# The last LayerNorm of a decoder layer taken under the last two expert tiles, its shift written to the output early and its scaled rows added there by DMA

## The chip, the cores and the metric

One core of a Trainium2 chip runs the whole layer as one launch. The metric is the device time of that launch in microseconds (us), the median of several executions. One execution was taken with the hardware profiler; its span and its trace are what the rows below come from.

## The reference, cut to what matters

One decoder layer over 1024 tokens of 1024 float32 values. Two attention branches and an output projection come first, then a LayerNorm, then a mixture of 32 experts of which each token uses two (both in one group of eight), then the last LayerNorm:

```python
h = layer_norm(ALPHA * h + mix, ln1_g[l], ln1_b[l])
ffn = hierarchical_moe(h, moe_w_group[l], moe_b_group[l], moe_w_router[l], moe_b_router[l],
                       moe_w_gate[l], moe_w_up[l], moe_w_down[l])
h = layer_norm(ALPHA * h + ffn, ln2_g[l], ln2_b[l])
```

`layer_norm` takes mean and variance over the 1024 values of a row, scales by the gain `ln2_g` and adds the shift `ln2_b`. A row of the output can be normed only when both of its experts have been added to it.

## The kernel before, in words

The code does not issue instructions directly. Calls on `V` (VectorE), `S` (ScalarE), `G` (GpSimd), `PE` (TensorE) and `LD` (SyncE, which issues DMAs) are recorded as tasks, and a list scheduler, `Sched.flush`, puts them into one fixed order for each engine. Therefore nearly every row of a profile names line 312, and rows are told apart by the names of the tiles. On the chip an engine works through its order and waits wherever the next instruction must wait.

**The expert stage.** The rows after the first LayerNorm lie in DRAM twice: in `h1_d` (to be read) and in `y_d` (to be added to). Tile t takes one expert's tokens (up to 128). `gather_x` brings their rows in with an indirect DMA that GpSimd issues, `x_tr` transposes them, `gate_up`, `hidden`, `hid_tr` and `down` do the gated MLP, and `scatter` adds the result to `y_d` with an indirect DMA with `compute_op=add`, also issued by GpSimd. The four views of `y_d` let scatters of different expert groups go without waiting for one another; a tile of another kind uses `y_d` as a whole and waits for all earlier scatters to land. There are 33 tiles: 32 experts, and one overflow tile for tokens beyond the 128 of an expert. Its weights are fetched by indirect DMAs from GpSimd. Should more tiles overflow, a loop with a count read on the chip (`For_i`) runs after the stage; it runs zero times here.

The weights are float32. An expert has three chunks of 1 MB, loaded by SyncE into a ring of eight buffers `rw`. `w_split` makes a high and a low part of each half chunk: ScalarE copies (`whg`, `whd`), VectorE subtracts (`wlg`, `wld`). A chunk's buffer is free for the next load when that is done. In the loop over t the pass for t does `gate_up(t)`, `hid_tr` and `down` of tile p = t - 1, the splits of t + 1, and the scatter of tile p - 1.

**The last stage.** After tile 32, the overflow tile, has been scattered, eight tiles `z` of 128 rows are loaded from `y_d`. `z_in` takes mean and variance of each on VectorE or ScalarE, small operations on GpSimd, ScalarE and VectorE make the factor, `z_out` applies gain and shift in one of three ways, and SyncE stores the rows to the output. The gain and the shift (`lnr`, 2 times 512 KB as each partition gets its own copy) are loaded behind the last weights.

Of the kernel before, what the change touches and what calls it, by code (L numbers as in the profile page):

```python
# [12 lines left out]
F32 = mybir.dt.float32  # L13
# [419 lines left out]
def layer_kernel(ctx, tc, x, meta, cst, rope, lnrows, gcol, small, wr_in, w_in, w_uq, w_ukv, w_o, w_e, c_bd, c_key, c_mask, out):  # L433
# [21 lines left out]
    o_d = dram.tile([NB, 128, 2, 1024], F32, name="o_d")  # L455
    h1_d = dram.tile([NB * 128, D], F32, name="h1_d")
    y_d = dram.tile([NB * 128, D], F32, name="y_d")

    def st(shape, dt=F32, name="s", bufs=2):
        return sm.tile(shape, dt, name=name, tag=name, bufs=bufs)  # L460
# [855 lines left out]

    nload, nsplit = [0], [0]

    def expert(t):
        return t % 4 * 8 + t // 4  # L1320

    def load_chunk(e, c, after=None):
        i = nload[0]
        if RA + RX <= i < RA + RX + 4:
            RAW[e, c] = [pq4.tile([128, 1024], F32, name="w4", tag="w4", bufs=8) for _ in range(2)]
            parts = [(RAW[e, c][q], q * 1024, (q + 1) * 1024) for q in range(2)]
        else:
# [9 lines left out]
        if e < NE:  # L1337
# [306 lines left out]
    XS, YS, GU, HD, OV = ({} for _ in range(5))  # L1644

    def ix(t):
        e = expert(t) if t < NE else NE
        return slice(e, e + 1)

    def gather_x(t):  # L1650
# [43 lines left out]
    def down(t, q):  # L1694
        hh, hl = HD[t]
        y = ps.tile([128, 512], F32, name="y", tag="y", bufs=4)
        for f in range(2):
            hi, lo = WS[t, 4 + f]
            c = slice(q * 512, (q + 1) * 512)
            mm3(y, (hh[:, f, :], hl[:, f, :]), (hi[:, c], lo[:, c]), f == 0, f == 1)  # L1700
        if q == 0:
            YS[t] = pq4.tile([128, D], F32, name="w4", tag="w4", bufs=8)
        copy_s(YS[t][:, q * 512:(q + 1) * 512], y)

    def scatter(t):
        G.indirect_dma_start(out=View(y_d, t % 4, 4) if t < NE else y_d, out_offset=Offsets(idxX[:, ix(t)]), in_=YS.pop(t), in_offset=None,
                             bounds_check=NB * 128 - 1, oob_is_err=False, compute_op=OP.add)

    def overflow_table():
        f = pb.tile([128, 7, NE], F32, name="ovf", tag="ovf", bufs=1)  # L1710
# [42 lines left out]
        V.memset(prevk, -1.0)  # L1753

    NT = NE + 1
    for i in range(GB4):
        gather_x(i)
    for _ in range(RB):
# [7 lines left out]
    for t in range(NT + 1):  # L1766
        p = t - 1
        cur, nxt = t < NT, t + 1 < NT
        if cur:
            gate_up(t, 0)  # L1770
            if t:
                w_split(t, 5)
                load_more()
            gate_up(t, 1)
        if nxt and t:
# [21 lines left out]
            WS.pop((p, 4)), WS.pop((p, 5))  # L1797
        if t + LEAD < NT and t:
            gather_x(t + LEAD)
        if p >= 1:  # L1800
            scatter(p - 1)
        if nxt:
            w_split(t + 1, 3)
            load_more()
            w_split(t + 1, 4)
        if t == 12:
            overflow_list()
        if t == 16:
            overflow_table()
    Y = {NT - 1: YS[NT - 1].t}  # L1810
    scatter(NT - 1)
    XS[NT] = None
    lnr = rawp.tile([128, 2, D], F32, name="rw", tag="rw", bufs=RA)
    for q in range(2):
        LD.dma_start(lnr[:, q, :], bc_row(4 + q))
    sched.flush()
    sched.direct = True
    global NAMES
# [3 lines left out]
    with tc.For_i(0, n_more, 1):  # L1822
# [14 lines left out]
        down(t, 0)  # L1837
        down(t, 1)
        scatter(t)
    b1.close()  # L1840
    aw.close()
    sched.direct = False
    sched.clock = dict.fromkeys(sched.clock, max(t.end for t in Y[NT - 1].users) + 1.0)


    with ExitStack() as c1:
        pb = c1.enter_context(pool("f"))
        Z, CF = {}, {}
        for n in range(NB):
            Z[n] = pb.tile([128, D], F32, name="z", tag="z", bufs=8)  # L1850
            LD.dma_start(Z[n], y_d[n * 128:(n + 1) * 128, :])

        def small(name, *shape):
            return pb.tile([128] + list(shape), F32, name=name, tag=name, bufs=8)

        def z_in(n):
            z = Z[n]
            m, v, r, t, nm = (small(f"z{i}", 1) for i in range(5))
            if n in AS:
                acc = small("za", 2)  # L1860
                junk = pb.tile([128, D], F32, name="zj", tag="zj", bufs=2)
                S.activation(junk, z, AF.Copy, accum_out=acc[:, 0:1])
                G.tensor_scalar(m, acc[:, 0:1], -1.0 / D, None, op0=OP.mult)
                S.activation(junk, z, AF.Square, bias=m, accum_out=acc[:, 1:2])
                sched.late = -ZL
                G.tensor_scalar(v, acc[:, 1:2], 1.0 / D, LN_EPS / ALPHA ** 2, op0=OP.mult, op1=OP.add)
            else:
                s6 = small("zs", 2, 6)
                mv = small("zv", 2)
                for q in range(2):  # L1870
                    ln_stats(z, s6, q)
                V.bn_aggr(mv, flat(s6))
                sched.late = -ZL
                G.tensor_scalar(v, mv[:, 1:2], LN_EPS / ALPHA ** 2, None, op0=OP.add)
                G.tensor_scalar(m, mv[:, 0:1], -1.0, None, op0=OP.mult)
            S.activation(r, v, AF.Sqrt)
            V.reciprocal(r, r)
            G.tensor_scalar(t, r, r, v, op0=OP.mult, op1=OP.mult)
            G.tensor_scalar(t, t, -0.5, 1.5, op0=OP.mult, op1=OP.add)
            G.tensor_tensor(r, r, t, op=OP.mult)  # L1880
            if "A" in OUT[n][0][0] + OUT[n][1][0]:
                G.tensor_tensor(nm, m, r, op=OP.mult)
            sched.late = 0.0
            CF[n] = m, r, nm

        def z_out(n):
            z, (m, r, nm) = Z[n], CF[n]
            for q in range(2):
                c = slice(q * 512, (q + 1) * 512)
                way, e1, e2 = OUT[n][q]  # L1890
                g, b = lnr[:, 0, c], lnr[:, 1, c]
                if way == "A":
                    S.activation(z[:, c], z[:, c], AF.Identity, bias=nm, scale=r)
                    e1.tensor_tensor(z[:, c], z[:, c], g, op=OP.mult)
                    e2.tensor_tensor(z[:, c], z[:, c], b, op=OP.add)
                else:
                    V.scalar_tensor_tensor(z[:, c], z[:, c], m, g, op0=OP.add, op1=OP.mult)
                    if way == "B":
                        V.scalar_tensor_tensor(z[:, c], z[:, c], r, b, op0=OP.mult, op1=OP.add)
                    else:  # L1900
                        S.activation(z[:, c], z[:, c], AF.Copy, scale=r)
                        e2.tensor_tensor(z[:, c], z[:, c], b, op=OP.add)
                if n in HS:
                    LD.dma_start(out[n * 128:(n + 1) * 128, c], z[:, c])
            if n not in HS:
                LD.dma_start(out[n * 128:(n + 1) * 128, :], z)

        AS, HS, ZL, ZLAG = (2, 3, 5, 6, 7), (2, 3, 4, 5, 6, 7), 0.2, 3
        A, B, C = ("A", V, V), ("B", V, V), ("C", V, G)
        OUT = (C, B), (B, C), (B, C), (("A", G, G), B), (B, B), (B, B), (C, B), (B, A)  # L1910
        for i in range(NB + ZLAG):
            if i < NB:
                z_in(i)
            if i >= ZLAG:
                z_out(i - ZLAG)
    sched.flush()
    sched.direct = True


def _constants():  # L1920
# [79 lines left out]
```

## Time and profile before

| | |
|---|---|
| median of 3 runs | 915.42 us (915.32 to 917.07) |
| the profiled execution, its own time | 913.97 us |
| its span, first to last instruction | 912.2 us |
| TensorE busy | 802.9 us, 88% |
| VectorE busy | 671.9 us, 74% |
| ScalarE busy | 514.4 us, 56% |
| GpSimd busy | 339.6 us, 37% |

The profiled execution lies 1.45 us under the median, and its span is 1.77 us shorter than its own time. Busy shares are averages over stages that differ much: the experts take from about 505 us to 866 us of the span, the last stage the rest.

### The profile page before, as it was taken

The page shows a single profiled execution, that of the slowest core. Times are in us where ns is not written, and L with a number is a line of the kernel's source. Part 1 is how long each engine was busy: PE and PEld are TensorE (multiplying, and loading weights), DVE is VectorE, ACT ScalarE, POOL GpSimd, SP SyncE. Part 2 cuts the span into 40 slices and gives each one's busy share as a digit, 9 for nine tenths or more (in the row PEclk, how much of TensorE's full clock was granted, in tenths as well). Part 3 has the DMA queues.
Part 4 walks back from the last instruction along what each step waited for, and adds up shares of the span by engine and source line. Part 5 has one row for each costly group of instructions (what it writes and reads, how often), then busy time and mean ns, then how long its engine had stood idle before and what let it go on. Part 6 is the DMA issues. An engine that isn't in the chain of part 4 may idle for free.

```text
span 912.2 us, 13596 instructions
## 1 busy us (share of the span) xinstructions
PE 802.9 (88%) x4616; PEld 687.0 (75%) x4616; DVE 671.9 (74%) x1336; ACT 514.4 (56%) x971; POOL 339.6 (37%) x605
## 2 busy tenths in 40 slices
PE   3899999999999999999997599999998998897700
PEld 2898998999999988888886488888777776675500
DVE  7946623888777656568667799999987787887447
ACT  3524422667656545412212599988777777777434
POOL 3757523344331215332214323433532333333147
PEclk9999999999999999999998699999999999999955
DMA  9444513121211112799956487999999999997154
GB/s 332 175 146 166 170 67 97 44 95 45 84 50 48 47 70 73 269 343 402 331 196 242 151 289 228 354 379 349 335 368 334 336 336 346 330 327 238 15 208 162
DMA packets 49863, 195.63 MB, mean 214 GB/s; under 512 B 12336, under 2 KB 13872, under 8 KB 37632
## 3 DMA queue, kind: packets, MB, share of 16 engines
q1 hardware_dynamic: 37552, 166.41, 49.4%
q0 software_dynamic: 12240, 28.34, 11.4%
q8 instruction: 37, 0.61, 0.3%
q14 instruction: 34, 0.28, 0.1%
HBM read 164.52 MB, written 48.01 MB: 233 GB/s over the span
## 4 chain that ended last, share of the span: by engine, by line
PE 59%; DMA 21%; DVE 9%; POOL 5%; issue 3%; ACT 2%; SPq 0%; POOLq 0%; ACTq 0%; DVEq 0%
PE sc L312 33%; DMA rw<-in_w_e_dram 17%; PE tr L312 9%; PE gu L312 8%; PE po L312 4%; PE y L312 4%; DVE wlg L312 3%; POOL z L312 2%; DVE wld L312 2%; DMA y_d<-w,idx 1%; POOL rsp L312 1%; DMA oT<-o_d 1%; ACT whg L312 1%; DMA z<-y_d 1%; DVE h L312 1%
## 5 line engine op out<-in xcount | busy, mean ns | idle before, releaser
L312 DVE TENSOR_TENSOR wlg<-rw,whg 128x1024 fp32r<-128x1024 f32 x120 | 142.9, 1219 | 37.6 <-ACT whg L312 37.0
L312 POOL DMA_INDIRECT y_d<-w,idx x33 | 76.9, 2330 | 226.4 <-ACT w L312 197.3
L312 ACT ACTIVATE whg<-rw 128x1024 fp32r<-128x1024 f32 x120 | 124.5, 1060 | 50.4 <-DMA rw<-in_w_e_dram 44.8
L312 PE MATMUL gu<-wlg,xh 128*128 128x512 f32 x264 | 106.9, 405 | 12.4 <-DVE wlg L312 12.3
L312 PE MATMUL sc<-wh,ht 128*128 128x448 f32 (+3 forms) x400 | 116.0, 371 | 1.9 <-DVE ht L312 1.3
L312 PE MATMUL gu<-whg,xh 128*128 128x512 f32 x264 | 109.3, 414 | 3.8 <-ACT whg L312 3.7
L312 PE MATMUL gu<-whg,xl 128*128 128x512 f32 x264 | 105.2, 398 | 1.5 <-DVE xl L312 1.5
L312 PEld LDWEIGHTS sc<-wh,ht 128*128 128x128 f32 x400 | 74.1, 192 | 9.6 <-DVE ht L312 1.8
L312 PEld LDWEIGHTS gu<-wlg,xh 128*128 128x128 f32 x264 | 50.2, 190 | 30.6 <-DVE wlg L312 20.5
L312 PE MATMUL sc<-wl,ht 128*128 128x448 f32 (+3 forms) x200 | 73.0, 365 | 0.0
L312 DVE TENSOR_TENSOR wld<-rw,whd 128x1024 fp32r<-128x1024 f32 x58 | 68.3, 1218 | 2.1 <-ACT whd L312 2.0
L312 PEld LDWEIGHTS gu<-whg,xh 128*128 128x128 f32 x264 | 50.3, 191 | 15.3 <-ACT whg L312 6.3
L312 PEld LDWEIGHTS gu<-whg,xl 128*128 128x128 f32 x264 | 50.4, 191 | 12.2 <-DVE xl L312 3.0
L312 ACT ACTIVATE whd<-rw 128x1024 fp32r<-128x1024 f32 x58 | 58.3, 1063 | 0.0
L312 PE MATMUL y<-whd,hl 128*128 128x512 f32 x124 | 49.3, 397 | 2.6 <-DVE hl L312 2.6
L312 PE MATMUL y<-whd,hh 128*128 128x512 f32 x124 | 51.5, 415 | 0.0
L312 PE MATMUL sc<-w,oT 128*128 128x512 f32 x192 | 49.8, 402 | 0.6 <-DMA oT<-o_d 0.6
L312 ACT ACTIVATE pt<-sc,ng 128x272 f32<-128x272 f32 (+9 forms) x56 | 29.9, 539 | 34.5 <-DVE ng L312 34.3
L312 PE MATMUL y<-wld,hh 128*128 128x512 f32 x124 | 49.3, 398 | 0.0
L312 PE MATMUL tr<-cs,w 128*128 128x128 f32 x264 | 40.8, 279 | 9.1 <-DMA w<-h_d,idx 7.4
L312 POOL DMA_INDIRECT w<-h_d,idx x33 | 43.6, 1321 | 11.2 <-issue 6.4
L312 PE MATMUL sc<-wo,oT 128*128 128x512 f32 x192 | 46.6, 392 | 0.0
(325 smaller groups left out, 1965.2 us busy)
## 6 DMA issues: line engine op xcount, KB each, us to landing
rw<-in_w_e_dram SPq DMA_DIRECT2D x88, 1024.0 KB, 21.4
o_d<-oT SPq DMA_DIRECT2D x16, 512.0 KB, 2.7
oT<-o_d POOLq DMA_DIRECT2D x16, 512.0 KB, 8.5
x<-in_w_in_dram SPq DMA_DIRECT2D x8, 672.0 KB, 6.2
u_d<-r SPq DMA_DIRECT2D x7, 672.0 KB, 3.3
h_d<-h SPq DMA_DIRECT2D x8, 512.0 KB, 3.2
hr<-h_d SPq DMA_DIRECT2D x8, 512.0 KB, 10.5
h_d<-hr SPq DMA_DIRECT2D x8, 512.0 KB, 5.0
```

Source lines behind the costliest of these rows:

```text
L312: inst = getattr(t.eng.real, method)(*[self.real(a) for a in args], **{k: self.real(v) for k, v in kw.items()})
```

## The change

- The overflow tile is no longer tile 32 but tile 24 (`OVP`), between the experts; the last expert is tile 32.
- The shift `ln2_b` is written into the output by eight DMAs from DRAM to DRAM, one in every second pass of the attention loop.
- `lnr` is loaded in the middle of the expert stage, into the buffer `rx`, which is free by then.
- When tile 30 has been scattered, `old_rows` gathers from `y_d` the rows that tiles 31 and 32 (`FIX` = 2) will change, and `norm_rows` loads all of `y_d`, takes mean and variance (four of the eight row tiles on VectorE, four on ScalarE), makes the factors four row tiles at a time on VectorE, multiplies with gain and factor in place, and adds the eight results to the output with indirect DMAs from GpSimd.
- Tiles 31 and 32 add their result to the gathered rows (VectorE, straight out of PSUM). `renorm` norms these rows once more, both with gain and shift, and an indirect DMA overwrites their rows in the output. That write comes after all eight additions have landed, the second one also after the first. Both tiles' rows are also written back to `y_d`.
- The former last stage is gone. The loop for further overflow tiles norms its own rows.

```diff
@@
+        if i % 2 and i < 2 * NB:
+            LD.dma_start(outs[i // 2 * 128:(i // 2 + 1) * 128, :], bc_row(5))
@@
+    OVP, FIX, NL = 24, 2, 0.0
+
     def expert(t):
+        t -= t > OVP
         return t % 4 * 8 + t // 4
@@
+        c = slice(q * 512, (q + 1) * 512)
+        if NT - FIX <= t < NT:
+            V.tensor_tensor(ZF[t][:, c], y, ZF[t][:, c], op=OP.add)
+            return
@@
+    def old_rows(t):
+        ZF[t] = pq4.tile([128, D], F32, name="w4", tag="w4", bufs=8)
+        G.indirect_dma_start(out=ZF[t], out_offset=None, in_=y_d, in_offset=Offsets(idxX[:, ix(t)]),
+                             bounds_check=NB * 128 - 1, oob_is_err=False)
...
+    def z_stat(z, mv, on_s):
+        if on_s:
+            acc = small("za", 3)
+            junk = pb.tile([128, 2048], F32, name="rb", tag="rb", bufs=RB)[:, 0:D]
+            S.activation(junk, z, AF.Copy, accum_out=acc[:, 0:1])
+            S.activation(acc[:, 1:2], acc[:, 0:1], AF.Copy, scale=-1.0 / D)
+            S.activation(junk, z, AF.Square, bias=acc[:, 1:2], accum_out=acc[:, 2:3])
...
+        else:
+            s6 = small("zs", 2, 6)
+            for q in range(2):
+                ln_stats(z, s6, q)
+            V.bn_aggr(mv, flat(s6))
...
+            elif way == "M":
+                V.scalar_tensor_tensor(dst[:, c], z[:, c], m, g, op0=OP.subtract, op1=OP.mult)
+                S.activation(dst[:, c], dst[:, c], AF.Copy, scale=r)
...
+    def norm_rows():
+        for n in range(NB):
+            z_load(n)
...
+        ZB = ((0, 4), (4, 8))
+        for n0, n1 in ZB:
+            mv = small("zv", 4, 2)
+            for n in range(n0, n1):
+                z_stat(Z[n], mv[:, n - n0, :], n in (2, 3, 6, 7))
+            r, nm = z_coef(mv[:, 0:n1 - n0, :], n1 - n0)
...
+                def store(c, n=n):
+                    G.indirect_dma_start(out=View(outs, n, NB), out_offset=Offsets(tokx[:, n:n + 1]), in_=Z[n], in_offset=None,
+                                         bounds_check=NB * 128 - 1, oob_is_err=False, compute_op=OP.add)
+                    STORES[len(STORES)] = sched.tasks[-1]
+                z_out(Z[n], Z[n], *ZC[n], 'MMMMMMMM'[n], (1, 1, 1, 1, 1, 1, 1, 1)[n], store)
...
+    def renorm(t):
+        mv = small("zv", 4, 2)
+        z_stat(ZF[t], mv[:, 0, :], False)
+        r, nm = z_coef(mv[:, 0:1, :], 1)
+        dst = pq4.tile([128, D], F32, name="w4", tag="w4", bufs=8)
+        z_out(dst, ZF[t], mv[:, 0, 0:1], r, nm, 'B', 2)
+        view = (t - (t > OVP)) % 4
+        G.indirect_dma_start(out=outs, out_offset=Offsets(idxX[:, ix(t)]), in_=dst, in_offset=None,
+                             bounds_check=NB * 128 - 1, oob_is_err=False)
+        for u in STORES.values():
+            sched.tasks[-1].preds[u] = u.lat
+        G.indirect_dma_start(out=View(y_d, view, 4), out_offset=Offsets(idxX[:, ix(t)]), in_=ZF[t], in_offset=None,
+                             bounds_check=NB * 128 - 1, oob_is_err=False)
@@
-        if p >= 1:
+        if 1 <= p < NT - FIX:
             scatter(p - 1)
+        if p == NT - FIX - 1:
+            scatter(p)
+            for i in range(NT - FIX, NT):
+                old_rows(i)
+        if p >= NT - FIX:
+            renorm(p)
@@
+        if p == NT - FIX - 1:
+            norm_rows()
         if t == 12:
             overflow_list()
+            for q in range(2):
+                LD.dma_start(lnr[:, q, :], bc_row(4 + q))
```

Three places of the fixed orders matter below. The first is the end of GpSimd's order. Before, it held the indirect loads of the overflow tile's weights (`rw`) and the scatters of tiles 28 to 32, the last of them `w_9806`:

```order
L312 DMA rw<-in_w_e_dram,widx 128x2048
L312 DMA y_d<-w_9488,idx 1024x1024
L312 DMA rw<-in_w_e_dram,widx 128x2048 x2
L312 DMA y_d<-w_9594,idx 1024x1024
L312 DMA y_d<-w_9717,idx 1024x1024
L312 DMA y_d<-w_9779,idx 1024x1024
L312 DMA y_d<-w_9806,idx 1024x1024
```

Now the last plain scatter is that of tile 30 (`w_9715`). `w_9771` and `w_9793` are the gathered rows of tiles 31 and 32, `w_9932` and `w_9966` the same rows after the second norm, `rw` with `tokx` the eight row tiles that are added to the output:

```order
L312 DMA y_d<-w_9715,idx 1024x1024
L312 DMA w_9771<-y_d,idx 128x1024
L312 DMA w_9793<-y_d,idx 128x1024
L312 DMA y_d<-w_9771,idx 1024x1024
L312 DMA out_dram<-rw,tokx 1024x1024 x8
L312 DMA y_d<-w_9793,idx 1024x1024
L312 DMA out_dram<-w_9932,idx 1024x1024
L312 DMA out_dram<-w_9966,idx 1024x1024
```

The two gathers stand behind the scatter whose result they read, and everything that writes the output stands behind them.

The second place is VectorE's order at the last two tiles. Before, the subtraction `hl` of tile 32 followed at once on the hidden layer `hid` of that tile, and nothing came after it until the last stage:

```order
L312 TENSOR_TENSOR wlg<-rw,whg 128x1024 x2
L312 TENSOR_TENSOR rv<-rw,rv 128x1024
L312 TENSOR_TENSOR xl<-tr,xh 128x512
L312 TENSOR_TENSOR rv<-rw,rv 128x1024
L312 TENSOR_TENSOR hl<-tr,hh 128x256
L312 SCALAR_TENSOR_TENSOR hid<-gu,wsl,sil 128x256
L312 TENSOR_TENSOR hl<-tr,hh 128x256
```

Now the addition to the gathered rows of tile 31 (`w_9771`) stands between them, and the statistics (`BN_STATS`, `BN_AGGR`) and the products with the gain of the eight row tiles follow:

```order
L312 TENSOR_TENSOR hl<-tr,hh 128x256
L312 SCALAR_TENSOR_TENSOR hid<-gu,wsl,sil 128x256
L312 TENSOR_TENSOR w_9771<-y,w_9771 128x512 x2
L312 TENSOR_TENSOR hl<-tr,hh 128x256
L312 BN_STATS zs<-rw 128x6 x3
L312 BN_AGGR zv<-zs 128x2
L312 BN_STATS zs<-rw 128x6
L312 SCALAR_TENSOR_TENSOR rw<-rw,zv,rx 128x1024
L312 BN_AGGR zv<-zs 128x2
L312 SCALAR_TENSOR_TENSOR rw<-rw,zv,rx 128x1024
```

So all of the norm's work on VectorE waits until the gathered rows of tile 31 are there.

The third place is SyncE's order from the middle of the expert stage on, as a piece of the difference (`kt` is a small table for the overflow tile):

```order
 L312 DMA rw<-in_w_e_dram 128x2048 x21
-L312 DMA kt_7235<-in_c_key_dram 128x448
+L312 DMA kt_7243<-in_c_key_dram 128x448
+L312 DMA rx<-in_lnrows_dram 128x1024 x2
 L312 DMA rw<-in_w_e_dram 128x2048 x59
-L312 DMA rw<-in_lnrows_dram 128x1024 x2
```

The two loads of gain and shift moved from behind the last 59 loads of weights to ahead of them.

## Rows read from the trace of the kernel before

**Rows 1.** Chain that ended last, in order of time: start us, us, what.

```profile
813.28 26.42 DMA rw<-in_w_e_dram
...
858.88 5.55 DMA y_d<-w,idx
...
866.23 4.59 DMA y_d<-w,idx
...
908.00 0.69 DVE z L312
```

**Rows 2.** Busy time by stretch: PE, PEld, DVE, ACT, POOL, granted clock, DMA share, GB/s.

```profile
680.00:820.00 140.00, 125.32 (x594) 98.58 (x595) 111.35 (x128) 104.27 (x152) 44.60 (x26) 1.00 0.96 336
...
875.00:913.00 38.00, 0.00 (x0) 0.00 (x0) 27.28 (x43) 16.66 (x34) 26.92 (x48) 0.50 0.54 202
```

**Rows 3.** Timeline of SyncE's DMA issues: start us, us, issue.

```profile
836.60 0.80 SPq L312 DMA_DIRECT2D rw<-in_lnrows_dram  x2
871.74 4.02 SPq L312 DMA_DIRECT2D z<-y_d  x8
```

**Rows 4.** Timeline of ScalarE, first chunk of a tile: start us, us, instruction, idle before.

```profile
817.01 2.01 ACT L312 ACTIVATE whg<-rw 128x1024 fp32r<-128x1024 f32 x2 [2.18 <-DMA rw<-in_w_e_dram]
```

**Rows 5.** Timeline of GpSimd, a gather behind a scatter and the last scatters.

```profile
782.97 1.03 POOL L312 DMA_INDIRECT w<-h_d,idx  x1 [0.30 <-issue]
...
813.40 2.46 POOL L312 DMA_INDIRECT y_d<-w,idx  x1 [7.35 <-ACT w L312]
...
823.87 2.47 POOL L312 DMA_INDIRECT y_d<-w,idx  x1 [6.67 <-ACT w L312]
...
850.45 1.58 POOL L312 DMA_INDIRECT y_d<-w,idx  x1 [11.25 <-ACT w L312]
858.88 1.56 POOL L312 DMA_INDIRECT y_d<-w,idx  x1 [6.85 <-ACT hh L312]
866.23 1.58 POOL L312 DMA_INDIRECT y_d<-w,idx  x1 [5.79 <-issue]
```

**Rows 6.** Scatters in 836 to 849 and in 850 to 858: issue to landing.

```profile
DMA to landing us min/median/max: 10.7/10.7/10.7
...
DMA to landing us min/median/max: 4.7/4.7/4.7
```

**Rows 7.** DMA issues of the page (median us to landing), and the first gather in the chain.

```profile
w<-h_d,idx POOLq DMA_INDIRECT x33, 11.8
...
507.22 5.22 DMA w<-h_d,idx
```

**Rows 8.** DMA queues, 620 to 820 and then 851 to 856: packets, MB, share of 16 engines.

```profile
q1 hardware_dynamic: 7904, 57.51, 75.6%
q0 software_dynamic: 5368, 10.37, 20.9%
...
q0 software_dynamic: 144, 0.12, 19.2%
```

**Rows 9.** Groups of VectorE and ScalarE, 870 us to the end: busy us, mean ns.

```profile
L312 DVE SCALAR_TENSOR_TENSOR z<-z,z,rw 128x512 f32<-128x512 f32 x24 | 20.8, 908 | 3.2 <-POOL z L312 3.2
L312 DVE BATCH_NORM_STATS2 zs<-z 128x6 f32<-128x512 f32 x6 | 3.8, 673 | 16.2 <-DMA z<-y_d 16.2
L312 DVE RECIPROCAL z<-z 128x1 f32<-128x1 f32 x8 | 1.2, 154 | 2.3 <-ACT z L312 2.2
L312 DVE BATCH_NORM_AGGREGATE zv<-zs 128x2 f32<-128x12 f32 x3 | 0.6, 200 | 0.0
L312 ACT ACTIVATE zj<-z,z 128x1024 f32<-128x1024 f32 x5 | 5.7, 1136 | 1.4 <-POOL z L312 1.4
```

**Rows 10.** Timeline of VectorE at the last split and at a 512-wide read from PSUM.

```profile
850.09 0.68 DVE L312 TENSOR_TENSOR xl<-tr,xh 128x512 fp32r<-128x512 f32 x1
850.69 1.21 DVE L312 TENSOR_TENSOR rv<-rw,rv 128x1024 fp32r<-128x1024 f32 x1
```

**Rows 11.** Stretch 85 to 250 us, attention, columns as in rows 2.

```profile
85.00:250.00 165.00, 163.37 (x1135) 151.22 (x1134) 108.11 (x299) 83.10 (x232) 67.05 (x176) 1.00 0.26 86
```

More of the change, by code (lines that the diff above doesn't have):

```diff
@@ L457, in layer_kernel @@
     y_d = dram.tile([NB * 128, D], F32, name="y_d")
+    outs = Tile(dram, (NB * 128, D), F32, "out", None, 1)
+    outs.ap = out
+    outs = outs.ref()
     def st(shape, dt=F32, name="s", bufs=2):
@@ L1336, in load_chunk @@
             G.tensor_copy(parts[0][0][:, 0:1], after)
-        if e < NE:
+        if e != OVP and e <= NE:
             r0 = expert(e) * 128
@@ L1646, in ix @@
     def ix(t):
-        e = expert(t) if t < NE else NE
+        e = expert(t) if t != OVP and t <= NE else NE
         return slice(e, e + 1)
@@ L1700, in down @@
             mm3(y, (hh[:, f, :], hl[:, f, :]), (hi[:, c], lo[:, c]), f == 0, f == 1)
+        c = slice(q * 512, (q + 1) * 512)
+        if NT - FIX <= t < NT:
+            V.tensor_tensor(ZF[t][:, c], y, ZF[t][:, c], op=OP.add)
+            return
         if q == 0:
             YS[t] = pq4.tile([128, D], F32, name="w4", tag="w4", bufs=8)
-        copy_s(YS[t][:, q * 512:(q + 1) * 512], y)
+        copy_s(YS[t][:, c], y)
     def scatter(t):
-        G.indirect_dma_start(out=View(y_d, t % 4, 4) if t < NE else y_d, out_offset=Offsets(idxX[:, ix(t)]), in_=YS.pop(t), in_offset=None,
+        own = t != OVP and t <= NE
@@ L1707, in scatter @@
+        G.indirect_dma_start(out=View(y_d, (t - (t > OVP)) % 4, 4) if own else y_d, out_offset=Offsets(idxX[:, ix(t)]), in_=YS.pop(t), in_offset=None,
                              bounds_check=NB * 128 - 1, oob_is_err=False, compute_op=OP.add)
+    def old_rows(t):
+        ZF[t] = pq4.tile([128, D], F32, name="w4", tag="w4", bufs=8)
+        G.indirect_dma_start(out=ZF[t], out_offset=None, in_=y_d, in_offset=Offsets(idxX[:, ix(t)]),
+                             bounds_check=NB * 128 - 1, oob_is_err=False)
@@ new lines, in layer_kernel, with small, z_load @@
+    Z, ZF, ZC, STORES = ({} for _ in range(4))
+    def small(name, *shape):
+        return pb.tile([128] + list(shape), F32, name=name, tag=name, bufs=2)
+    def z_load(n):
+        if n % 2 == 0:
+            Z["pair"] = rawp.tile([128, 2048], F32, name="rw", tag="rw", bufs=RA)
+        Z[n] = Z["pair"][:, n % 2 * D:(n % 2 + 1) * D]
+        LD.dma_start(Z[n], y_d[n * 128:(n + 1) * 128, :])
+    def z_stat(z, mv, on_s):
[5 more added lines that the diff above has]
+            S.activation(junk, z, AF.Square, bias=acc[:, 1:2], accum_out=acc[:, 2:3])
+            S.activation(mv[:, 0:1], acc[:, 0:1], AF.Copy, scale=1.0 / D)
+            S.activation(mv[:, 1:2], acc[:, 2:3], AF.Copy, scale=1.0 / D)
+        else:
[3 more added lines that the diff above has]
+            V.bn_aggr(mv, flat(s6))
@@ new lines, in z_out @@
+    def z_out(dst, z, m, r, nm, way, parts, store=None):
+        w = D // parts
+        for q in range(parts):
+            c = slice(q * w, (q + 1) * w)
+            g, b = lnr[:, 0, c], lnr[:, 1, c]
+            if way == "N":
+                S.activation(dst[:, c], z[:, c], AF.Identity, bias=nm, scale=r)
+                V.tensor_tensor(dst[:, c], dst[:, c], g, op=OP.mult)
+            elif way == "M":
+                V.scalar_tensor_tensor(dst[:, c], z[:, c], m, g, op0=OP.subtract, op1=OP.mult)
+                S.activation(dst[:, c], dst[:, c], AF.Copy, scale=r)
+            elif way == "A":
+                S.activation(dst[:, c], z[:, c], AF.Identity, bias=nm, scale=r)
+                V.tensor_tensor(dst[:, c], dst[:, c], g, op=OP.mult)
+                V.tensor_tensor(dst[:, c], dst[:, c], b, op=OP.add)
+            else:
+                V.scalar_tensor_tensor(dst[:, c], z[:, c], m, g, op0=OP.subtract, op1=OP.mult)
+                V.scalar_tensor_tensor(dst[:, c], dst[:, c], r, b, op0=OP.mult, op1=OP.add)
+            if store:
+                store(c)
@@ L1755, in layer_kernel @@
     NT = NE + 1
+    lnr = rawp.tile([128, 2048], F32, name="rx", tag="rx", bufs=RX).rearrange("p (a b) -> p a b", a=2)
     for i in range(GB4):
@@ L1770, in layer_kernel @@
             gate_up(t, 0)
+            if 0 < t < NT - 1:
+                w_split(t, 5)
             if t:
-                w_split(t, 5)
                 load_more()
@@ L1805, in layer_kernel @@
             w_split(t + 1, 4)
+        if t == NT - 2:
+            w_split(t + 1, 5)
+        if p == NT - FIX - 1:
+            norm_rows()
         if t == 12:
             overflow_list()
+            for q in range(2):
+                LD.dma_start(lnr[:, q, :], bc_row(4 + q))
         if t == 16:
             overflow_table()
-    Y = {NT - 1: YS[NT - 1].t}
-    scatter(NT - 1)
     XS[NT] = None
-    lnr = rawp.tile([128, 2, D], F32, name="rw", tag="rw", bufs=RA)
-    for q in range(2):
-        LD.dma_start(lnr[:, q, :], bc_row(4 + q))
     sched.flush()
@@ L1839, in layer_kernel @@
         scatter(t)
+        old_rows(t)
+        mv = small("zv", 4, 2)
+        z_stat(ZF[t], mv[:, 0, :], False)
+        r, nm = z_coef(mv[:, 0:1, :], 1)
+        z_out(ZF[t], ZF[t], mv[:, 0, 0:1], r, nm, "B", 1)
+        G.indirect_dma_start(out=out, out_offset=Offsets(idxX[:, ix(t)]), in_=ZF[t], in_offset=None,
+                             bounds_check=NB * 128 - 1, oob_is_err=False)
     b1.close()
     aw.close()
-    sched.direct = False
-    sched.clock = dict.fromkeys(sched.clock, max(t.end for t in Y[NT - 1].users) + 1.0)
@@ L1846, in layer_kernel @@
[L1846 to L1915, printed above, removed]
@@ L1916, in layer_kernel @@
-    sched.flush()
-    sched.direct = True
 def _constants():
```

19 lines of the change are left out of this document (added).

## The prediction, made before the changed kernel was run

> **What bounds the kernel now.** I read the chain of work that ended last first, because the change touches only what comes at the end. From 813 us on it is the last direct load of weights (26.42 us from issue to landing, so until 839.7), then matmuls, then two scatters one behind the other, and from 871.74 the last stage with nothing under it, whose last VectorE instruction begins at 908.00 [rows 1, 3]. The busy times by stretch say why the weights stand there: from 680 to 820 us the DMA engines are busy for 0.96 of the time at 336 GB/s, while PE has 125 us of work in 140 [rows 2]. So the expert stage is bound by its loads. In the last stage no engine is full: VectorE 27.28, GpSimd 26.92 and ScalarE 16.66 us of 38 [rows 2]; it is a chain of small waits, 912.2 - 871.7 = 40.5 us long.
>
> The change starts the norm earlier but makes a new chain. What counts is when the scatter of tile 30 lands, since the new loads and gathers all wait for it, and how long that chain is to the end. I follow it in the span's time.
>
> **Step 1, the stream of weights.** The two loads of `lnr` were behind the weights, at 836.60 [rows 3], where nobody was waiting. Now they are ahead of 59 loads in the stage that is bound by DMA: 1.05 MB at 336 GB/s, 3.1 us later for all that follows. The overflow tile has the same bytes at either place, so it shifts nothing here. The eight writes of the shift into the output (4.2 MB) fall into attention, where PE is busy for 163.4 of 165 us and the DMA engines only for 0.26 [rows 11]. I cost them at nothing; if one stood ahead of a load that PE waits for, 0.52 MB at 336 GB/s would be 1.6 us.
>
> **Step 2, the scatter of tile 30.** In the steady part a scatter starts 6.9 us after ScalarE starts on the first chunk of the tile two further on: 817.01 to 823.87 [rows 4, 5]. That chunk is of tile 30 at 817.01. Tile 32 is two tiles further, at the 10.9 us that the stage takes for a tile (scatters from 813.40 to 823.87 are 10.5 apart; 3.15 MB of weights and 0.5 MB of rows at 336 GB/s are 10.9): 817.0 + 21.8 + 3.1 = 841.9, scatter at 848.8. When no new loads come behind the last, the rest arrives faster; then VectorE's and PE's own work holds, 125 of 140 us, 9.8 a tile: 817.0 + 19.6 + 3.1 + 6.9 = 846.6. I take 847.5; before it was 850.45 [rows 5]. So putting the overflow tile in the middle gives only 3 us here. What it gives besides is that tile 32 no longer needs a scatter of its own that waits for tile 31 (858.88, then 866.23).
>
> **Step 3, until the norm's rows are there.** A scatter lands 4.7 us after its issue with idle DMA engines and 10.7 under load [rows 6]. The weights are through by then, but tile 30 may have more rows: 6.5 us, 854.0. SyncE then issues the eight loads of `y_d`, 18 us earlier than before (871.74). GpSimd starts an indirect DMA about 1.8 us after the landing that it waits for (858.88 + 5.55 = 864.4, next at 866.23 [rows 1, 5]): the gather of tile 31 starts at 855.8. A gather takes 5.22 us with little else under way and 11.8 in the median, under load [rows 7]; beside the eight loads I take 9: 864.8.
>
> **Step 4, VectorE.** Its order puts the addition of tile 31 ahead of everything of the norm, so all of it starts at 864.8, and the norm is hardly under the last two tiles. Ahead of the first factor stand: two additions out of PSUM (0.68 each [rows 10]), one `hl` (0.4), nine statistics (0.673), four aggregates (0.2), eight products of 128x1024, and some twelve small operations (0.154) [rows 9]. A product of 1024 is not in the trace: a two-operand one of that width takes 1.21 [rows 10], two of 512 with GpSimd beside them 1.82 [rows 9]; 1.25, since GpSimd does no arithmetic now (bound 1.82: 4.6 us more). Sum: 1.4 + 0.4 + 6.1 + 0.8 + 10.0 + 1.8 = 20.5, first factor at 885.3. ScalarE's first product (1.14 [rows 9]) and 0.3 to GpSimd: first addition at 886.7. ScalarE's four statistics, about 2.6 us each [rows 9], end behind the last load at some 875 and lie under this.
>
> **Step 5, eight additions by DMA, 128 rows each.** No row shows one this large. GpSimd needs 1.58 us for a scatter when DMA is idle and 0.3 between two [rows 5], so from below: 7 x 1.88 + 5.55 to land = 18.7 us. But the engines must also do the adding. Over 200 us the software queue took 20.9% of them for 10.37 MB [rows 8], half of it gathers, half scatters. If gathers go at the rate of the hardware queue (57.51 MB in 75.6%, 380 GB/s), they took 13.6 of 41.8 us, and the scatters 28.2 for 5.19 MB, 184 GB/s. An addition of 0.52 MB is then 2.85 us of all engines, eight are 22.8; with 1.6 ahead and 1 behind, 25.4. From above: the scatter after 850 cost 19.2% of 5 us for 0.12 MB [rows 8], 125 GB/s or 4.2 us each, 36 in all. I take 25.4, last landing at 912.1.
>
> The Trainium skill's page "DMA: Bandwidth & Descriptors" (section "Anatomy of one DMA") fits a GpSimd DMA as 2.0 us plus its bytes at 436 GB/s and names no surcharge for adding. By it one of these is an estimated 3.2 us and eight would follow GpSimd's pace, 18.7 rather than 25.4. The rows on scatters speak against it, since by them adding halves the rate or worse.
>
> **Step 6, the two last writes.** `w_9932` goes when all eight have landed, `w_9966` when `w_9932` has: twice 1.8 + 4.7 = 13.0, 925.1. These are plain writes of few rows, not additions; from below 0.9 (SyncE's wait at 870.8 to 871.74 [rows 1, 3]) and 3.6 each, 9.0 in all. The loop of no passes, which lay between scatter and load before (those 0.9 us), now stands at the end; with the 1.5 us that the span ran on after the last store: 927.5.
>
> The rest of VectorE's order (the factor of the second four, both second norms, some 14 us after the first factor) ends near 900, under the additions.
>
> **Sum.** Against the span of 912.2: scatter of tile 30 3 us earlier, and from it to the end 80 instead of 61.8 us, 15.3 us more. Own time 913.97 + 15.3 = 929.3; the median of the runs lies 1.45 above it, 930.7. A difference under 0.2% (1.8 us) can't be told from none with this kernel.
>
> **The rivals.**
> *The software queue at its quiet prices.* Gather 5.2, additions at GpSimd's pace, short last writes, scatter at 846.6 and landing in 4.7: 846.6 + 4.7 + 0.9 + 5.2 + 20.5 + 1.4 + 18.7 + 9.0 + 2.4 = 909.4 in the span, 912.6 as a median, 0.3% faster than now. For it: DMA is nearly idle after 846. Against: eight loads of 0.5 MB run beside the gather, and scatters with idle engines did cost 125 GB/s. It decides if the train from the first addition's start to the last landing is under some 20 us and the gather under 6. With the rule of the page above it would come out this way. Chance 0.22.
> *Additions at the isolated price.* 36 us instead of 25.4, or products at 1.82: 935 to 945. Chance 0.18.
> *The start is missed.* If the tail of the stream is as fast as its bytes (a scatter at 843, say) all else being as forecast, 926; this stays in the forecast's range, as does a gather at 11.8 (933).
> *Between.* Quiet additions with the rest as forecast give 924; quiet additions and a quiet gather with long waits 918, about no change. Chance of within 0.2%: 0.08.
>
> **How the numbers follow.** The forecast, slower, 919 to 937, has 0.52. With the isolated price slower is 0.70, faster 0.22, same 0.08. The likeliest is 930. The range runs from 910, which takes in most of the quiet rival, to 942, short of the case in which all upper bounds meet (10.7, 11.8, 1.82 and 36 together, about 950).
>
> **What would show it.** Right: SyncE's loads of `y_d` near 855, VectorE idle from about 850 until the gather of tile 31 has landed, the eight additions ending at GpSimd some 15 to 25 us after the first, and GpSimd then waiting for DMA twice at the end. Wrong: the loads of `y_d` at 845 or before, additions that land within 19 us, statistics that run while PE still works, or an end set by VectorE. The same price error in adding by DMA (2.85 us each) moves the end by 8 us for each us, so this is what can make it wrong most.

## The result and the profile after

| | before | after |
|---|---|---|
| device time, median | 915.58 us (4 runs, 915.32 to 917.07) | 921.93 us (4 runs, 920.84 to 922.66) |
| ratio to before | 1 | 1.0072, 95% interval 1.0056 to 1.0087 |
| profiled execution: span / own time | 912.2 / 913.97 us | 920.8 / 922.66 us |

The change made the kernel 0.7% slower. The forecast was 930.0, 1.6% slower: the sign was right, the size was more than twice too large. The spans differ by 8.6 us and the medians by 6.35, since the profiled execution of before lay 1.6 us under its median and that of after 0.7 us above it.

First, GpSimd's timeline of the changed kernel (start us, us, instruction, idle time before it and what ended it). It answers to [rows 5].

```profile
846.89 1.98 POOL L312 DMA_INDIRECT y_d<-w,idx  x1 [6.75 <-ACT w L312]
854.37 1.06 POOL L312 DMA_INDIRECT w<-y_d,idx  x1 [5.49 <-PE y L312]
...
881.88 1.62 POOL L312 DMA_INDIRECT out_dram<-rw,tokx  x1 [11.98 <-ACT rw L312]
883.80 1.59 POOL L312 DMA_INDIRECT out_dram<-rw,tokx  x1 [0.30 <-ACT rw L312]
...
895.42 1.56 POOL L312 DMA_INDIRECT out_dram<-rw,tokx  x1 [0.30 <-issue]
897.28 1.02 POOL L312 DMA_INDIRECT y_d<-w,idx  x1 [0.30 <-issue]
908.02 1.00 POOL L312 DMA_INDIRECT out_dram<-w,idx  x1 [9.72 <-DMA out_dram<-rw,tokx]
911.40 0.97 POOL L312 DMA_INDIRECT out_dram<-w,idx  x1 [2.38 <-DMA out_dram<-w,idx]
```

From top to bottom: the scatter of tile 30 (850.45 before), the gather of tile 31, the first two and the last of the eight additions, the write that puts tile 31's rows back into `y_d`, and the two last writes. GpSimd has issued everything by 898.3, and then stands idle for 9.72 us, because the additions that it issued have not landed. The chain that ended last names that time (start us, us, what), in answer to [rows 1]:

```profile
895.42 11.70 DMA out_dram<-rw,tokx
...
908.02 2.61 DMA out_dram<-w,idx
```

VectorE's timeline shows what is ahead of it:

```profile
852.08 0.48 DVE L312 SCALAR_TENSOR_TENSOR hid<-gu,wsl,sil 128x256 f32<-128x256 f32 x1 [0.65 <-ACT sil L312]
862.29 1.29 DVE L312 TENSOR_TENSOR w<-y,w 128x512 f32<-128x512 f32 x2 [9.72 <-DMA w<-y_d,idx]
863.49 0.42 DVE L312 TENSOR_TENSOR hl<-tr,hh 128x256 fp32r<-128x256 f32 x1
...
876.61 1.28 DVE L312 SCALAR_TENSOR_TENSOR rw<-rw,zv,rx 128x1024 f32<-128x1024 f32 x1
877.81 0.15 DVE L312 SCALAR_TENSOR_TENSOR z<-z,z 128x4 f32<-128x4 f32 x1
...
880.27 0.16 DVE L312 SCALAR_TENSOR_TENSOR z<-zv,z 128x4 f32<-128x4 f32 x1
```

It stands for 9.72 us, too, until the gather of tile 31 has landed (862.29), and from there works without a gap to the first factor (880.27). SyncE's loads of `y_d` start 18 us earlier than in [rows 3]:

```profile
853.59 3.80 SPq L312 DMA_DIRECT2D rw<-y_d  x8
```

The busy times by stretch (PE, PEld, VectorE, ScalarE, GpSimd, granted clock, DMA share, GB/s), in answer to the last of [rows 2]:

```profile
865.00:885.00 20.00, 3.18 (x10) 2.20 (x8) 19.96 (x52) 11.26 (x22) 3.83 (x3) 0.59 0.14 36
885.00:905.00 20.00, 0.00 (x0) 0.00 (x0) 6.53 (x25) 3.70 (x4) 11.17 (x8) 0.50 1.06 202
```

The end is two stages one behind the other: first VectorE is full and the DMA engines are nearly idle (0.14), then the DMA engines are full (1.06; this share can pass 1) at only 202 GB/s and the others wait. In the stage of before no engine was full in 38 us [rows 2]; computing and storing lay beside each other there.

What SyncE waited for at the program's last line, in the changed kernel and then in the one before (us in total, times, longest):

```profile
SPq L2052 <- PEq L2052: 5.6, 2, 5.1
```

```profile
SPq L1996 <- DMA out_dram<-z: 1.5, 2, 1.2
SPq L1996 <- PEq L1996: 0.7, 2, 0.5
```

The last write, issued at 911.40, lands 3.0 us later, at 914.4; the span ends at 920.8, so 6.4 us behind it. In the kernel before, that was 1.5 us.

The profile puts SyncE's wait down to PE's sequencer, but PE is done there by 915.6. What runs on is an instruction named DRAIN, which every engine has at the program's last line. GpSimd's longest one, in the changed kernel and then in the one before (how often, ns, start us):

```profile
L2052 POOLq DRAIN  x1: 4771/4771/4771, 915.2 to 915.2; - x1
```

```profile
L1996 POOLq DRAIN  x1: 5671/5671/5671, 905.6 to 905.6; - x1
```

In the changed kernel it starts when the last write has landed and ends at 920.0, and SyncE goes on at 920.2. Before, it started under the last stores and ended at 911.3, 0.6 us behind the last landing. In all traces of this case the span ends 0.8 to 1.1 us behind GpSimd's DRAIN.

### The profile page after: what moved, and what is told of

It reads as the page before. It is cut to its first block, busy times and chain, and to the rows that moved or that the text cites. A ratio compares the mean times of both kernels' runs of the same rounds, so it can differ in the third digit from the quotient of the medians.

```text
span 920.8 us, 13580 instructions
## 1 busy us (share of the span) xinstructions
PE 803.1 (87%) x4616; PEld 686.5 (75%) x4616; DVE 674.7 (73%) x1372; ACT 514.2 (56%) x968; POOL 322.4 (35%) x569
## 4 chain that ended last, share of the span: by engine, by line
PE 54%; issue 23%; POOL 9%; DMA 8%; DVE 4%; ACT 1%; SPq 1%; POOLq 0%
PE sc L312 32%; PE tr L312 8%; PE gu L312 6%; PE po L312 4%; DMA y_d<-w,idx 3%; PE y L312 3%; POOL w L312 2%; POOL y_d L312 2%; DMA out_dram<-rw,tokx 1%; DMA rw<-y_d 1%; POOL rsp L312 1%; POOL out_dram L312 1%; DMA oT<-o_d 1%; DVE h L312 1%; SPq L312 1%
## 5 line engine op out<-in xcount | busy, mean ns | idle before, releaser
L312 POOL DMA_INDIRECT y_d<-w,idx x33 | 69.6, 2108 | 222.5 <-ACT w L312 182.3
L312 DVE TENSOR_TENSOR xl<-tr,xh 128x512 fp32r<-128x512 f32 x66 | 45.2, 684 | 5.2 <-ACT xh L312 4.9
## 6 DMA issues: line engine op xcount, KB each, us to landing
rw<-in_w_e_dram SPq DMA_DIRECT2D x88, 1024.0 KB, 20.8
```

The lines of the kernel that those rows point to most:

```text
L312: inst = getattr(t.eng.real, method)(*[self.real(a) for a in args], **{k: self.real(v) for k, v in kw.items()})
```

## The experiments

Each ratio is to the kernel before on the same chip (its median there 914.1 to 914.8), and ratios are compared. The theory: the norm's chain, not engine time, sets the end, and its greatest piece is that adding by DMA keeps the DMA engines busy. The rivals: GpSimd's issuing, the moved loop, or the early loads.

**Without the adding.** Edit: `e1_plain_writes` is the changed kernel with the row tiles written plainly, which leaves the shift out of the output:

```diff
-  bounds_check=NB * 128 - 1, oob_is_err=False, compute_op=OP.add)
+  bounds_check=NB * 128 - 1, oob_is_err=False)
```

> The changed kernel with the eight row tiles written to the output plainly instead of added there; this leaves the shift out of the rows. Theory A, the forecast's step 5: the adding itself occupies the DMA engines, 2.85 us a row tile, which made the 25.2 us from the first addition's start to the last landing. Plain writes of 0.52 MB at 380 GB/s are 1.4 us each, so GpSimd's pace holds (1.0 us as in the two last writes, plus 0.3): 7 x 1.3 + 3 = 12 us, end about 13 us earlier, median near 909. Rival B, the train is set by GpSimd's issuing (1.57 + 0.3 each) and by the latency of a landing under load (11 us): still 20 us or more, median 916 or above.

Measured: 910.29, ratio 0.9963 (0.9950 to 0.9977). The first and the last of the eight writes in GpSimd's timeline:

```profile
880.79 1.00 POOL L312 DMA_INDIRECT out_dram<-rw,tokx  x1 [11.87 <-ACT rw L312]
...
890.54 1.08 POOL L312 DMA_INDIRECT out_dram<-rw,tokx  x1 [0.30 <-issue]
```

The landings of all eight in its group of DMA issues (median us):

```profile
out_dram<-rw,tokx POOLq DMA_INDIRECT x8, 3.9
```

The same group in the changed kernel:

```profile
out_dram<-rw,tokx POOLq DMA_INDIRECT x8, 9.9
```

From the first start to the last landing (890.54 + 4.25) the train takes 14.0 us, with additions 25.24 (881.88 to 907.12): adding costs 11.2 us. Theory A holds. Plain writes follow GpSimd, 1.3 to 1.6 us apart. The same bytes (4.19 MB) went at 300 GB/s plainly and at 166 as additions.

**Without the loop.** `e2_no_loop` is the changed kernel, `e4_before_no_loop` the one before, each without the loop over further overflow tiles (which has no pass here):

```diff
-    n_more = nc.values_load(nov[0:1, 0:1].real(), min_val=0, max_val=15, ...)
-    with tc.For_i(0, n_more, 1):
-        ...
```

> The changed kernel without the loop for further overflow tiles, which makes no pass with these inputs. Theory A: the 6.4 us between the landing of the last write and the end of the span are the jump over the loop, which all engines make together; without it 1.5 us as in the kernel before, so 5 us less, median near 917. Rival B: they are the wait for the completion of the writes to the output: change under 1 us, 921 to 922.

> The kernel before without the loop for further overflow tiles. Theory A: there the jump over the loop lies under the last stage for all engines but SyncE, so at most the 0.9 us between the landing of the last scatter and the first load of the last stage are saved: 914.5 to 915.6. Rival B: the jump costs 5 us wherever it stands: near 910.5.

Measured: 920.67, ratio 1.0070 (1.0052 to 1.0088), and 913.76, ratio 0.9993 (0.9979 to 1.0007). At either place the loop's cost can't be told from none. In the trace the changed kernel still ends 4.8 us behind the last landing (910.93 + 3.0, span 918.7), with SyncE at the last line waiting for PE's sequencer:

```profile
SPq L2025 <- PEq L2025: 4.4, 2, 3.9
```

With the loop it was 6.4, so the loop has 1.6 us of the long end and is not what makes it long. GpSimd's DRAIN is still there, from 910.7 to 917.9.

**Only the overflow tile moved.** `e3_before_ovp24` is the kernel before with the overflow tile as tile 24:

```diff
+    OVP = 24
     def expert(t):
+        t -= t > OVP
         return t % 4 * 8 + t // 4
-        if e < NE:
+        if e != OVP and e <= NE:
```

(`ix` and `scatter` get the same test.)

> The kernel before with one part of the change, the overflow tile as tile 24 instead of last; last stage and gain and shift as before. Theory A: besides the few us by which the stream's tail comes earlier, the last scatter no longer waits for the one before it to land (858.88 to 866.23 in the kernel before), and the loads of the last stage start near 863 instead of 871.7: median 906 to 908. Rival B, as the forecast had it for step 2: the stream of weights ends where it did and the gain is 3 us or less, 912 to 915.

Measured: 904.31, ratio 0.9887 (0.9868 to 0.9906), faster than both kernels and than either theory had it. (Its profiled execution was the slowest of six, 907.94; its rows are read for the order of things.) GpSimd's last scatters and SyncE's loads of `y_d`:

```profile
845.25 1.98 POOL L312 DMA_INDIRECT y_d<-w,idx  x1 [6.75 <-ACT w L312]
853.65 1.55 POOL L312 DMA_INDIRECT y_d<-w,idx  x1 [6.43 <-ACT hh L312]
858.05 1.57 POOL L312 DMA_INDIRECT y_d<-w,idx  x1 [2.85 <-ACTq L1826]
...
864.33 5.50 SPq L312 DMA_DIRECT2D z<-y_d  x8
```

Against [rows 5] the last scatter starts at 858.05 instead of 866.23, since it no longer waits for the landing of the one ahead. This part of the change alone gains 10 us, and the rest of it, from 0.9887 to 1.0072, costs 17.

**The loads of `lnr` late.** `e5_late_lnr` is the changed kernel with the two loads behind all but six weight loads:

```diff
         if p == NT - FIX - 1:
+            for q in range(2):
+                LD.dma_start(lnr[:, q, :], bc_row(4 + q))
             norm_rows()
         if t == 12:
             overflow_list()
-            for q in range(2):
-                LD.dma_start(lnr[:, q, :], bc_row(4 + q))
```

> The changed kernel with the two loads of lnr behind all but six of the weight loads on SyncE instead of ahead of 59 of them; nothing else differs. Theory A (the stage is bound by its loads, and those two cost what the traces of the changed kernel and of e3 differ by): the scatter of tile 30 starts 1.6 us earlier, at 845.3 instead of 846.9, all behind it moves with it, ratio 1.0055 to the kernel before instead of 1.0072. Rival B (the forecast's price, their bytes at 336 GB/s): 3.1 us earlier, 1.004. Rival C (the tail is set by PE and VectorE, not by loads): nothing, 1.007.

Measured: 919.75, ratio 1.0068 (1.0050 to 1.0086). In the trace the scatter of tile 30 starts at 844.74 instead of 846.89, 2.15 us earlier, and the first addition at 879.06 instead of 881.88. The two executions had entered the expert stage 0.46 us apart (first gather at 507.73 and 508.19); counted from there the scatter is 1.7 us earlier. The times can't tell 0.0004 from nothing: the trace puts the price between A and B, the ratio nearer to C. It stays open, and is small.

**The norm ahead of tiles 31 and 32 on VectorE.** `e6_norm_first`, the changed kernel with a later place for the additions to the gathered rows:

```diff
+            sched.late = 6.0
             V.tensor_tensor(ZF[t][:, c], y, ZF[t][:, c], op=OP.add)
+            sched.late = 0.0
```

> The changed kernel with the additions of tiles 31 and 32 to their gathered rows put behind the statistics and the products of the norm on VectorE, so that these needn't wait for the gather of tile 31. Theory A (the gather holds the norm, as step 4 of the forecast says): VectorE starts on the first loaded rows at about 858 instead of 862.3, the first addition to the output starts 3 to 4.5 us earlier, ratio 1.0025 to 1.004. Rival B (the loads of y_d run beside the gather and are no earlier, or ScalarE's statistics hold the first factor): less than 1 us, 1.007. Rival C (the second norms of tiles 31 and 32 come too late and their last writes wait for VectorE instead of for the additions): slower than the changed kernel, over 1.008.

Measured: 916.40, ratio 1.0036 (1.0019 to 1.0052). VectorE's first statistics and GpSimd's first and last addition and the write behind them:

```profile
856.47 1.29 DVE L312 BATCH_NORM_STATS2 zs<-rw 128x6 f32<-128x512 f32 x2 [1.50 <-DMA rw<-y_d]
...
875.84 1.64 POOL L312 DMA_INDIRECT out_dram<-rw,tokx  x1 [19.75 <-ACT rw L312]
...
889.46 1.77 POOL L312 DMA_INDIRECT out_dram<-rw,tokx  x1 [0.30 <-issue]
...
902.10 1.00 POOL L312 DMA_INDIRECT out_dram<-w,idx  x1 [9.53 <-DMA out_dram<-rw,tokx]
```

VectorE's wait is 1.50 us instead of 9.72, the train starts 6.0 us earlier, and is as long as before (875.84 to 901.11, 25.3 us). Theory A holds: the gather of tile 31 held up the whole norm. With the other order the loss against the kernel before falls from 0.72% to 0.36%.

**The norm without additions.** `e7_norm_complete`, the changed kernel with gain and shift on VectorE and stores by SyncE:

```diff
-            LD.dma_start(outs[i // 2 * 128:(i // 2 + 1) * 128, :], bc_row(5))
-                    G.indirect_dma_start(out=View(outs, n, NB), ..., compute_op=OP.add)
+                    LD.dma_start(outs[n * 128:(n + 1) * 128, c], Z[n][:, c])
-                z_out(Z[n], Z[n], *ZC[n], 'MMMMMMMM'[n], ..., store)
+                z_out(Z[n], Z[n], *ZC[n], 'BBBBBBBB'[n], 1, store)
```

> The changed kernel with the shift added on VectorE and the eight row tiles stored by SyncE, without the early writes of the shift and without additions in DMA; the output is complete. Theory A (the additions by DMA are the greatest loss of the change, 11.2 us of 25.2 by e1, and the rest of the train is GpSimd's pace): VectorE has 8 more operations of about 1.25 us behind the first factor at 880, the stores follow it at that pace and the last of the eight lands near 895; the last two writes behind VectorE's second norms at 897 to 905, end near 910, ratio 0.995 to 0.999. Rival B (VectorE becomes the bound, its second norms stand behind the eight products): the last write is near 912 and the end at 917, ratio 1.003. Either is above the 0.9887 of the kernel before with the overflow tile in the middle, if the norm under the last two tiles brings nothing.

Measured: 912.93, ratio 0.9986 (0.9973 to 0.9998). VectorE's eight second products take 4.86 us per four:

```profile
880.68 4.86 DVE L312 SCALAR_TENSOR_TENSOR rw<-rw,z,rx 128x1024 f32<-128x1024 f32 x4
...
888.83 4.86 DVE L312 SCALAR_TENSOR_TENSOR rw<-rw,z,rx 128x1024 f32<-128x1024 f32 x4
```

So 9.7 us of work more on VectorE cost less than the additions that they replace: 8 us were gained, as theory A had it. (The early writes of the shift and ScalarE's eight products are gone here too.)

**The last store on GpSimd.** `e8_last_on_gpsimd` is e3 with its very last store issued by GpSimd, a plain one:

```diff
-  LD.dma_start(out[n * 128:(n + 1) * 128, c], z[:, c])
+  (G if (n, q) == (NB - 1, 1) else LD).dma_start(out[n * 128:(n + 1) * 128, c], z[:, c])
```

> The kernel of e3 (before, with only the overflow tile as tile 24) with the very last store issued by GpSimd instead of SyncE. Theory A (the 4.8 to 6.4 us from the last landing to the end of the changed kernel come from a last DMA on GpSimd's queue): the end is 3 to 5 us later than e3's, ratio 0.992 to 0.994 instead of 0.9887. Rival B (what lies behind the last landing in the changed kernel is due to the indirect writes or to other engines' last work): less than 1 us, ratio 0.988 to 0.990.

Measured: 909.48, ratio 0.9954 (0.9941 to 0.9968), 5 us above e3 by the medians and 6 by the ratios. GpSimd's issue in its timeline, the median landing in the group of DMA issues, and SyncE's waits at the last line:

```profile
900.77 0.68 POOL L312 DMA_DIRECT2D out_dram<-z  x1 [1.57 <-DVE z L312]
```

```profile
out_dram<-z POOLq DMA_DIRECT2D x1, 256.0 KB, 2.8
```

```profile
SPq L2000 <- PEq L2000: 4.0, 2, 3.5
```

The same wait in e3:

```profile
SPq L2000 <- PEq L2000: 0.9, 2, 0.5
```

GpSimd's DRAIN in e8 and then in e3:

```profile
L2000 POOLq DRAIN  x1: 6401/6401/6401, 900.7 to 900.7; - x1
```

```profile
L2000 POOLq DRAIN  x1: 5672/5672/5672, 899.6 to 899.6; - x1
```

The end is 4.4 us behind the last landing (900.77 + 2.8 to 908.0), in e3 1.4 (902.7 + 2.0 to 906.1). One small store that goes by GpSimd instead of SyncE therefore brings most of the changed kernel's long end: the DRAIN, which in e3 lay under the last stores and ended at 905.3, now ends at 907.1 with nothing beside it for its last 3.6 us. The kernel loses more than theory A had it (0.992 to 0.994); of the 5 us, 3.0 are the longer end and 0.8 the longer landing, the rest is not traced. Whether late arithmetic on GpSimd would cost the same was not tried.

**Three edits together.** `e9_three_together` is e7 with the edits of e5 and e6.

> The kernel of e7 (complete norm, stores by SyncE) with the order of e6 (additions of tiles 31 and 32 to their gathered rows behind the statistics and products) and the late loads of lnr of e5. Theory A (the three gains lie behind one another on one chain and add up: from e7's 0.9986, 5 us less for the order, 1 to 2 us for lnr): about 906 to 907, ratio 0.991, slower than the kernel before with only the overflow tile moved (0.9887), so the norm under the last two tiles gives nothing here even without its additions by DMA. Rival B (the norm under the last two tiles pays once its own chain is short): below 0.987. Rival C (VectorE or the second norms are the bound by then): above 0.995.

Measured: 908.33, ratio 0.9934 (0.9916 to 0.9953), between A and C. VectorE is busy for 40.37 us of 43.00:

```profile
854.93:897.93 43.00, 1.19 (x6) 0.65 (x4) 40.37 (x86) 10.97 (x28) 2.99 (x3) 0.55 0.48 190
```

The last write is issued at 898.19 when VectorE is done, so VectorE sets when the last write goes. B falls: even without its additions, with a short chain, the norm under the last two tiles doesn't reach the kernel that only moves the overflow tile. But the last write lands at some 901.0 (2.8 us later) and the span ends at 907.0, 6 us behind it, against 1.4 in e3; GpSimd's DRAIN runs from 902.0 to 906.1. That difference, 4.6 us, is as large as the one between the two medians (4.0). What e9 loses against e3 thus has the size of the longer end, and whether the norm under the tiles would pay without it was not tried.

**The last writes as additions.** `e10_adding_last_writes` is the changed kernel with `compute_op=OP.add` in `renorm`'s write to the output; rows of tiles 31 and 32 come out otherwise.

> The changed kernel with the two last writes (normed rows of tiles 31 and 32) issued as additions instead of plain writes, which changes the output in those rows. It tests the step of the forecast that failed, where the two writes were priced from accumulating scatters at 1.8 + 4.7 us each, 13.0 in all, and took 3.4 + 3.0 = 6.4 us from the first one's start to the last landing. Theory A (that price was wrong because these writes don't add): as additions each starts later behind GpSimd's work and lands in 4 to 5 us, 9 to 12 us from the first one's start to the last landing, ratio 1.010 to 1.013. Rival B (they are short because they carry few rows, adding or not): under 7.5 us, ratio 1.007 to 1.009.

Measured: 926.36, ratio 1.0121 (1.0094 to 1.0148). GpSimd's timeline, and the median landing of the two:

```profile
908.94 1.55 POOL L312 DMA_INDIRECT out_dram<-w,idx  x1 [9.94 <-DMA out_dram<-rw,tokx]
914.17 1.56 POOL L312 DMA_INDIRECT out_dram<-w,idx  x1 [3.68 <-DMA out_dram<-w,idx]
```

```profile
out_dram<-w,idx POOLq DMA_INDIRECT x2, 4.9
```

The first lands in 4.47 us and the second in 5.3: from 908.94 to 919.5 are 10.6 us, against 6.4 as plain writes. Theory A holds: the same rows by the same engine cost 4.2 us more if they are added.

## Why the prediction was right in sign and wrong in size

| step of the forecast | forecast us | measured us |
|---|---|---|
| scatter of tile 30 starts | at 847.5 | at 846.89 |
| its landing | 6.5 | 6.5 |
| landing (853.4) to the gather's start | 1.8 | 0.97 |
| gather of tile 31 | 9.0 | 7.9 |
| VectorE to the first factor | 20.5 | 18.0 |
| to the first addition | 1.4 | 1.6 |
| eight additions | 25.4 | 25.24 |
| two last writes | 13.0 | 7.3 |
| from there to the end | 2.4 | 6.4 |
| span | 927.5 | 920.8 |

**Mechanism: right.** The order of events is that of the forecast: loads of `y_d` at 853.6, VectorE idle until the gather has landed, additions that end long behind GpSimd's issuing, two waits of GpSimd at the end. The quiet rival (909.4 in the span) wanted the train under 20 us and the gather under 6; they took 25.24 and 7.9. The rival of dearer additions wanted 36 us or products at 1.82; the products took 1.28. One of the forecast's signs of being wrong did come: VectorE's statistics (from 863.83) run while PE still works. PE had waited 8.38 us for the subtraction `hl` of tile 32, which stands behind the addition that waits for the gather, and did that tile's last matmuls from 863.96 to 868.2. Nothing on the chain to the end waited for them.

**Step 6 failed.** It says that the two last writes "are plain writes of few rows, not additions", and yet prices them by the accumulating scatters of before, twice 1.8 + 4.7 = 13.0 us. This is the term that was furthest off. They took 7.3: 0.9 until the first one starts, 2.61 to land, 0.77 until the second starts, 3.0 to land. The forecast's lower bound for them, 9.0, was above this too; the 3.6 us in it for a landing come from no row that it names. e10 shows that the missing addition is the cause: as additions the same writes make the kernel 0.5% slower still. In the same step the end was priced from SyncE's last store, 2.4 us; it took 6.4, of which 4.77 are GpSimd's DRAIN, which the forecast did not have, and e8 shows that a last DMA by GpSimd does most of that. These two errors have opposite signs and leave 1.7 us of the span's miss of 6.7; the rest comes from the steps ahead, below, and from the scatter of tile 30 (0.6).

So part of the forecast's nearness is luck. With the end as it was priced, the changed kernel would stand 4.0 us lower, at some 918, 0.3% above before, hardly more than the 0.2% that the forecast itself called noise.

**Steps 3 and 4 were each somewhat too dear.** The start of the gather (0.8) and its landing (1.1) came earlier. VectorE's 2.5 us are an error of adding up: its 37 instructions ahead of the first factor are, but for one small one, those that the forecast counted, and their durations sum to 20.9 us, near the forecast's 20.5, but they fill only 18.0. In the timeline above a product of 1.28 us that starts at 876.61 is followed by the next instruction at 877.81, 1.20 later. Durations of instructions that stand close together overlap by some 0.08 us here, which over 37 makes 2.9 us that a sum counts twice.

**The offset.** The forecast added 1.45 us to the profiled execution's own time, by which before lay under its median. After's profiled execution lay 0.7 above its own. These 2.1 us and the 6.7 of the span are the 8.8 between 930.7 and 921.93.

**Step 5 was right**, with some luck in its parts. 184 GB/s for adding, worked out from the share of the software queue, and 2.6 us around it gave 25.4 us. 25.24 were measured, with 202 GB/s in the full stretch (20.8 us for the eight) and 4.5 us around it. By the Trainium skill's page "DMA: Bandwidth & Descriptors" (section "Anatomy of one DMA", 2.0 us plus bytes at 436 GB/s) 0.52 MB would take an estimated 3.2 us. The first plain write of e1, with none ahead of it, landed in 3.3 us and agrees; the first addition of the changed kernel landed in 6.1 and does not, and the measurement decides. The medians of 3.9 and 9.9 hold the waiting behind earlier ones too.

**Steps 1 and 2.** The early loads of `lnr` delay the scatter of tile 30 by 1.6 us (against e3's at 845.25) to 2.15 (e5), or 1.4 and 1.7 counted from the expert stage's first gather, not by 3.1; this is by traces alone. The early writes of the shift show no cost: the expert stage's first gather starts at 508.19 in the changed kernel and at 507.22 in the one before [rows 7], but at 506.85 and 506.75 in e1 and e2, which have them, and at 507.98 in e3, which has not. That the overflow tile "gives only 3 us here" was right for the scatter of tile 30 with the loads of `lnr` ahead of it (3.6; in e3, without them, 5.2). The forecast named its other gain, tile 32 without a wait for tile 31, but gave it no price; by e3 the two are worth 10 us together, which the norm's longer chain takes back and 7 us more.

## What to carry to other kernels

Try the parts of such a change one by one: here moving one tile is the fastest kernel (0.9887), and starting the last stage earlier made it longer than the time it began ahead. Before adding in DMA in order to spare an engine, compare what the DMA engines take for it with what the engine would: 11.2 us against 9.7 on VectorE, on a chain where both are waited for. Price a DMA from one of its own kind and queue: the landing of the second of the last writes went from 3.0 to 5.3 us with nothing changed but the adding. Look in the trace at what stands between the last landing and the end of the span before moving the last work to another engine; here GpSimd's DRAIN, which lay under SyncE's stores before, came out and cost some 5 us.

## What the runs showed of the hardware that was not expected

- A last DMA issued by GpSimd leaves 4.4 us (one plain store, e8) to 6.4 us (the changed kernel) between its landing and the end of the span; a last store by SyncE 1.4 to 1.5. What fills it is GpSimd's DRAIN at the program's last line, which ends 3.6 us (e8) to 5.6 us (the changed kernel) behind that landing. In the kernel before and in e3, where arithmetic is GpSimd's last work, it ends 3.9 us behind that, for the most part under SyncE's last stores. Why it takes this long stays open.
- An indirect DMA that adds also takes GpSimd longer to issue: 1.56 to 1.95 us against 0.98 to 1.29 for the same rows written plainly.
- Additions queue up: GpSimd runs 1.86 us apart, and the landings fall behind up to 11.7 us, with the DMA engines at 1.06 busy and 202 GB/s (885 to 905 us).
